# Queries and keys of a prompt attention stored in split form: the split at the eviction, with the sums' scaling on VectorE

## The chip, the cores and the metric

The kernel runs on one core of a Trainium2 chip. The metric is device time in microseconds (us) of one execution, lower is better. The kernel before takes 3180.88 us as the median of 3 runs (3177.26 to 3182.94).

## The reference

One inference step of a decoder layer, all in 32-bit floats: 2048 prompt tokens and 8 x 8 sampled tokens with 8192 cached positions each. One input projection feeds eight heads of attention with a forget gate (FoX) and four heads of a matrix memory (mLSTM); their outputs are mixed by w_o, and a norm, a squared-ReLU MLP and a norm follow. What the change touches is the attention of the prompt:

```python
z  = x @ w_in                                  # 1024 columns in; queries and keys of FoX are 512 each
fq, fk, fv = z[..., :512], z[..., 512:1024], z[..., 1024:1536]      # 8 heads x 64
L  = cumsum(log_sigmoid(forget gate))
s  = (fq . fk) * 64**-0.5 + L[q] - L[k]        # keys up to the query
o  = softmax(s) . fv
# mLSTM, in chunks: C_new = g_state * C + sum(w_key k v),  g_state = exp(...)
mix = concat(o, norm(mLSTM) * og) @ w_o;  x1 = LN(ALPHA*x + mix)
y   = LN(ALPHA*x1 + square(relu(x1 @ w1)) @ w2)
```

`k_prompt`, the plain keys, is one of the outputs.

## The kernel before

**Split products.** TensorE multiplies in a rounded 32-bit form. A product that must be exact is made of parts: ScalarE copies a tile into the rounded form (the high part, `split_hi`, L154), VectorE subtracts it from the tile (the low part, `split_lo`, L157), and TensorE adds the products of the parts (`mm3`, L163 to L165). For the attention's scores a head has only 64 dimensions, so keys stand twice on 128 partitions: the high part in the upper 64 and the low part in the lower 64 of one tile `ks`, and one matmul of 128 partitions multiplies a part of the queries with both parts of the keys. Queries stand twice for this, too, in `qh` and `ql`.

**Stages.** The execution goes through these stages in order.

- `block_a`, four times (512 prompt tokens each, the first with the 64 sampled ones): the input projection in passes of 256 columns. Each pass loads its weights on SP's queue (`wra`), splits them (`whi`, `wlo`), and evicts its banks `pm`. The FoX queries and keys are passes with eight groups j of 128 columns, four of queries, four of keys. ScalarE evicts them in pieces of 256 tokens (L634, queries scaled by 0.125) into one of four buffers `st`, and SP stores them, queries to a scratch `dq`, keys to the output `k_prompt`. In the first block the sampled columns stand ahead of them in a bank of 320.
- `m_block`, woven into the next block's matmuls: the mLSTM chunks of a finished block. Four decays per block come from a scratch `dgs` into `gsb`; ScalarE exponentiates them at L741, ahead of the block's first chunk; the state's update at the end of a chunk uses them.
- the sampled attention, in small steps woven between the other stages' matmuls by `tick`. Its gathers of cached keys and values are DMAs on POOL's queue.
- `phase_b`, the prompt attention: eight heads, one after the other, each in eight units g of 256 queries (two query tiles of 128). `scores` makes a unit's banks `pS` (two matmuls each, `qh` and `ql` against `ks`), and VectorE adds the decay row `nl` and takes the maximum. `values` exponentiates on ScalarE, turns the result on TensorE, and multiplies with the values `vn`. The values of a unit are issued behind the scores of the next (LA = 1). ScalarE and VectorE bring the result into `ot` (L1105, L1107), one buffer of 1024 queries for four units.
- `phase_o`, the output projection with the first norm, then `phase_c`, the MLP. Their rows x come on SP's queue (L1345), as do the mixed rows `xr` (L1318) and the first weights `wr` of w_o (L1247, five of which are loaded in the last units of the attention already).

**The loads of the attention.** All go through SP's queue, in program order. Query tiles (`qn`, 128 x 256, twice the same 64 rows) are loaded two units ahead and split behind the scores of the unit before. The four key pieces of the next head (`kn`, 128 x 512) are loaded in units 0 to 3 (head 0's own and head 1's at other places) and split two units later. The next head's `nl` (1 MB) and `vn` (512 KB) are loaded in unit 3, behind its scores. Beside these, POOL's queue carries the additions `dw` that prepare the MLP's weights (`w2_sum`), with the accumulation done by the DMA; a counter spreads them over the units.

**The end of four units.** `finish` inverts the sums of the exponentials and puts three steps into the list `ends`; each of the next units starts with one of them. `stores` writes the inverses to a scratch (four small DMAs on SP), `sums` reads them back along the queries, on 64 partitions (`rl`, two DMAs), and `scale` multiplies the two halves of `ot` with them on POOL (L1133) and stores them to `dmix` (L1134, SP). For the last four units all steps follow at once: VectorE scales the first half, POOL the second, and POOL's queue stores both. There are two buffers `ot`.

The order of the work is that of the program on each engine; tile pools set when a buffer comes free. DMAs of SP's queue have eight semaphores in turn, so that a DMA also waits for the one eight places ahead of it.

## Time and profile before

| what | value |
|---|---|
| median of 3 runs | 3180.88 us |
| the profiled execution, its own time | 3166.91 us |
| its span in the profile | 3165.1 us, granted clock 0.990 |
| TensorE (PE) busy | 97% of the span |
| VectorE (DVE), ScalarE (ACT), GpSimd (POOL) busy | 67%, 46%, 30% |
| projections and mLSTM, sampled attention beside them | 0 to 865 us |
| prompt attention, eight heads | 865 to 1304.4 us |
| output projection and first norm | 1304.4 to about 1540 us |
| MLP and second norm | the rest |

Times in the trace run from the start of the span. A group of the profile is a line of the program, an engine, an operation, and its tiles as out<-in; busy us and the mean ns of one follow, then the idle time of the engine just ahead of these instructions and what ended it. A matmul's end is modelled, so "busy" TensorE includes matmuls that are a little stretched. The waits have the waiting engine on the left and what it waited for on the right, then us in sum, the count and the longest.

### The profile page before, as it was taken

The page shows a single profiled execution, that of the slowest core. Times are in us where ns is not written, and L with a number is a line of the kernel's source. Part 1 is how long each engine was busy: PE and PEld are TensorE (multiplying, and loading weights), DVE is VectorE, ACT ScalarE, POOL GpSimd, SP SyncE. Part 2 cuts the span into 40 slices and gives each one's busy share as a digit, 9 for nine tenths or more (in the row PEclk, how much of TensorE's full clock was granted, in tenths as well). Part 3 has the DMA queues.
Part 4 walks back from the last instruction along what each step waited for, and adds up shares of the span by engine and source line. Part 5 has one row for each costly group of instructions (what it writes and reads, how often), then busy time and mean ns, then how long its engine had stood idle before and what let it go on. Part 6 is the DMA issues. An engine that isn't in the chain of part 4 may idle for free.

```text
span 3165.1 us, 53757 instructions
## 1 busy us (share of the span) xinstructions
PE 3076.4 (97%) x19713; PEld 2425.7 (77%) x19713; DVE 2125.0 (67%) x5095; ACT 1457.3 (46%) x2648; POOL 961.5 (30%) x1046
## 2 busy tenths in 40 slices
PE   8999999999999999899999999999999999999998
PEld 8997787787766676677777777776777776798886
DVE  6857557466487888544566668665676656787888
ACT  4343244334377777422334354443454444455552
POOL 0121232333333334376423334324333222111110
PEclk9999999999999999999999999999999999999999
DMA  5565775777787787487977778978778866587772
GB/s 193 152 212 179 238 234 188 277 267 250 238 269 196 210 211 172 159 303 261 359 277 271 279 274 302 344 263 315 282 280 325 317 226 238 156 266 200 210 203 77
DMA packets 332512, 765.36 MB, mean 242 GB/s; under 512 B 64057, under 2 KB 154681, under 8 KB 331353
## 3 DMA queue, kind: packets, MB, share of 16 engines
q1 hardware_dynamic: 236120, 414.41, 39.9%
q0 software_dynamic: 90864, 330.61, 31.4%
q10 hardware_dynamic: 5264, 16.91, 1.4%
q8 instruction: 156, 2.56, 0.3%
q14 instruction: 108, 0.88, 0.1%
HBM read 709.23 MB, written 93.98 MB: 254 GB/s over the span
## 4 chain that ended last, share of the span: by engine, by line
PE 76%; DMA 11%; issue 5%; DVE 5%; POOL 2%; ACT 1%; SPq 0%; DVEq 0%; POOLq 0%; ACTq 0%
PE py L163 6%; PE py L165 6%; PE ph L163 6%; PE ph L165 6%; PE py L164 6%; PE ph L164 6%; PE pw L1359 5%; PE pm L163 5%; PE pm L165 5%; PE pm L164 5%; DMA y<-cache_v,idxV 3%; PE sO L2245 3%; PE po L1097 3%; DMA vt<-cache_v,idxV 3%; PE sQ L2132 3%
## 5 line engine op out<-in xcount | busy, mean ns | idle before, releaser
L157 DVE TENSOR_TENSOR wl<-wr,wh 128x1024 fp32r<-128x1024 f32 x321 | 393.5, 1230 | 237.3 <-ACT wh L154 235.7
L154 ACT ACTIVATE wh<-wr 128x1024 fp32r<-128x1024 f32 x321 | 337.6, 1055 | 326.0 <-PE ph L164 168.9
L2109 POOL DMA_INDIRECT kT<-cache_k,idxK x256 | 276.5, 1080 | 642.7 <-PE sQ L2132 576.4
L163 PE MATMUL py<-wh,hh 128*128 128x512 f32 x904 | 357.6, 400 | 0.1
L164 PE MATMUL py<-wl,hh 128*128 128x512 f32 x904 | 353.7, 393 | 0.0
L165 PE MATMUL py<-wh,hl 128*128 128x512 f32 x904 | 352.6, 394 | 0.8 <-DVE hl L157 0.8
L1668 DVE TENSOR_TENSOR y<-y,py 128x512 f32<-128x512 f32 x404 | 272.4, 681 | 84.5 <-PE py L165 81.4
L163 PE MATMUL ph<-x1h,wh 128*128 128x512 f32 x768 | 303.8, 396 | 0.0
L2221 POOL DMA_INDIRECT vt<-cache_v,idxV x197 | 203.2, 1032 | 329.8 <-PE sO L2245 257.4
L164 PE MATMUL ph<-x1l,wh 128*128 128x512 f32 x768 | 301.5, 393 | 0.0
L165 PE MATMUL ph<-x1h,wl 128*128 128x512 f32 x768 | 299.9, 393 | 0.0
L163 PE MATMUL pm<-xh,whi 128*128 128x512 f32 (+2 forms) x640 | 231.0, 361 | 0.0
L165 PE MATMUL pm<-xh,wlo 128*128 128x512 f32 (+2 forms) x640 | 228.8, 357 | 0.0
L164 PE MATMUL pm<-xl,whi 128*128 128x512 f32 (+2 forms) x640 | 227.9, 356 | 0.0
L163 PE MATMUL pm<-whi,xh 128*128 128x256 f32 (+4 forms) x624 | 202.1, 325 | 8.0 <-ACT whi L154 8.0
L157 DVE TENSOR_TENSOR wlo<-wra,whi 128x1024 fp32r<-128x1024 f32 (+1 forms) x112 | 141.0, 1261 | 101.1 <-ACT whi L154 100.8
L163 PEld LDWEIGHTS py<-wh,hh 128*128 128x128 f32 x904 | 169.4, 188 | 50.0 <-issue 5.9
L165 PEld LDWEIGHTS py<-wh,hl 128*128 128x128 f32 x904 | 170.1, 188 | 41.5 <-issue 4.9
L164 PE MATMUL pm<-wlo,xh 128*128 128x256 f32 (+4 forms) x624 | 199.5, 320 | 0.6 <-DVE wlo L157 0.6
L165 PE MATMUL pm<-whi,xl 128*128 128x256 f32 (+4 forms) x624 | 199.9, 320 | 0.0
L164 PEld LDWEIGHTS py<-wl,hh 128*128 128x128 f32 x904 | 170.5, 189 | 35.2 <-issue 2.5
L154 ACT ACTIVATE hh<-hq 128x512 fp32r<-128x512 f32 x150 | 94.1, 631 | 215.4 <-PE py L164 150.6
(442 smaller groups left out, 7210.5 us busy)
## 6 DMA issues: line engine op xcount, KB each, us to landing
wr<-w SPq DMA_DIRECT2D x214, 512.0 KB
wra<-w_in SPq DMA_DIRECT2D x104, 512.0 KB
wr<-dw SPq DMA_DIRECT2D x97, 512.0 KB
dw<-w POOLq DMA_DIRECT2D x63, 512.0 KB, 8.6
wr<-w POOLq DMA_DIRECT2D x34, 512.0 KB, 8.4
Rb<-dR SPq DMA_DIRECT2D x128, 128.0 KB
wx<-dw SPq DMA_DIRECT2D x17, 512.0 KB
xn<-xp_t SPq DMA_DIRECT2D x16, 512.0 KB
```

The costliest lines, as they stand in the source:

```text
L154: last["ACT"] = A.activation(dst, src, AF.Copy, scale=scale)
L157: r = (eng or V).tensor_tensor(dst, src, hi.bitcast(F32), op=OP.subtract)
L163: T.matmul(ps, wh, xh, start=first, stop=False, skip_group_check=shared)
L164: T.matmul(ps, wh, xl, start=False, stop=False, skip_group_check=shared)
L165: last["PE"] = T.matmul(ps, wl, xh, start=False, stop=stop, skip_group_check=shared)
L1097: last["PE"] = T.matmul(po[c:c + 64, q0:], z["vn"][:, k], PTs[k // 4][:, k % 4, q0:], start=(k < 2), stop=(k >= nk - 2), skip_group_check= ...
L1359: last["PE"] = T.matmul(ps, m[t][x][:, k], (wh, wl)[w][hf][k], start=i == 0, stop=i == 23)
L1668: V.tensor_tensor(y, y, ps, op=op)
L2109: G.indirect_dma_start(out=piece(n), out_offset=None, in_=ck, in_offset=IO(ap=idxK[:, b, j // 2, j % 2:j % 2 + 1], axis=0))
L2132: r = T.matmul(pq[h4 * 32:h4 * 32 + 32, hg].rearrange("p (k c) -> p k c", k=2), z["qb"][:, hd], kv, start=(db == 0), stop=(db == 1), skip_ ...
L2221: vx["last"] = G.indirect_dma_start(out=vt.rearrange("p f c -> p (f c)"), out_offset=None, in_=cv, in_offset=IO(ap=idxV[:, b, (kt % 4) * 4 ...
L2245: after_ = T.matmul(po[r:r + 32], z["PT"][:, hg, 2 * f + g, pg].rearrange("p h q -> p (h q)"), vts[f][:, g, hg * 256:(hg + 1) * 256], star ...
```

## The change

The change has four parts.

1. The scratch `dq` becomes two planes, high and low part, and a scratch `dk` of the same form is added for keys. The projection's eviction writes the high part on ScalarE (whole, 512 or 256 columns, L639 of the new program) and the low part on VectorE (`scalar_tensor_tensor`, scale times bank minus high part), and SP stores both. The plain keys are still copied and stored to `k_prompt`. The new tiles share the buffers of two others of that stage (tags `ac` and `qi`).
2. The attention loads finished parts: `ks` in place (high part to the upper, low part to the lower 64 partitions), and one tile `q` of 128 x 2 x 256 with both parts. `split_hi`, `split_lo`, `kn`, `qn`, `qh` and `ql` go. The next head's `nl` and `vn` are loaded in unit 4, behind its scores, no longer in unit 3.
3. VectorE scales all the sums; an empty step stands ahead of `scale` in `ends`, so it comes a unit later; `ot` has three buffers.
4. The exponential of `gsb` is issued behind the first chunk's outputs.

```diff
-    dq = drm.tile([4, 128, S], F32, name="dq")
+    dq = drm.tile([2, 512, S], F32, name="dq")
+    dk = drm.tile([2, 512, S], F32, name="dk")
...
+    def q_of(h, g):
+        return dap(dq, h * 64 * S + g * 256, [[S, 64], [512 * S, 2], [1, 256]])
...
-                for o in range(w % 256, w, 256):
-                    st = pa.tile([128, 256], F32, name="st", bufs=4)
-                    A.activation(st, ps[:, o:o + 256], AF.Copy, scale=scale)
-                    SY.dma_start(O["k_prompt"][jj * 128:(jj + 1) * 128, a:a + 256] if c else dq[jj, :, a:a + 256], st)
+                n = w // 256 * 256
+                hi = pa.tile([128, 512], F32, name="sa", tag="ac", bufs=2)[:, :n].bitcast(F32R)
+                lo = pa.tile([128, 512], F32, name="sq", tag="qi", bufs=2)[:, :n].bitcast(F32R)
+                A.activation(hi, ps[:, w - n:], AF.Copy, scale=scale)
+                V.scalar_tensor_tensor(lo, ps[:, w - n:], scale, hi.bitcast(F32), op0=OP.mult, op1=OP.subtract)
+                for d, x in enumerate((hi, lo)):
+                    SY.dma_start((dk if c else dq)[d, jj * 128:(jj + 1) * 128, a:a + n], x.bitcast(F32))
+                for o in range(w - n, w, 256):
+                    if c:
+                        st = pa.tile([128, 256], F32, name="st", bufs=4)
+                        A.copy(st, ps[:, o:o + 256])
+                        SY.dma_start(O["k_prompt"][jj * 128:(jj + 1) * 128, a:a + 256], st)
                     a += 256
...
-        A.activation(gsb, gsb, AF.Exp)
...
+            if c % 4 == 0:
+                A.activation(gsb, gsb, AF.Exp)
...
+        def keys_load(z, g):
+            h = z["h"]
             for d in range(2):
-                SY.dma_start(kn[d * 64:d * 64 + 64], kp[h * 64:h * 64 + 64, g * 512:(g + 1) * 512])
+                SY.dma_start(z["ks"][g][d * 64:d * 64 + 64].bitcast(F32), dk[d, h * 64:h * 64 + 64, g * 512:(g + 1) * 512])
...
-            k = z["ks"][:, g * 512:(g + 1) * 512]
-            split_hi(k, kn)
-            split_lo(k[64:128], kn[64:128], k[64:128])
...
-            qn = qns.pop() if qns else pb.tile([128, 256], F32, name="qn", bufs=3)
+            q = qs.pop() if qs else pb.tile([128, 2, 256], F32R, name="q", bufs=3)
             for d in range(2):
-                SY.dma_start(qn[d * 64:d * 64 + 64], dq[h // 2, h % 2 * 64:h % 2 * 64 + 64, g * 256:(g + 1) * 256])
+                SY.dma_start(q[d * 64:d * 64 + 64].bitcast(F32), q_of(*units[n]))
...
-            split_hi(qh, qn)
-            split_lo(ql, qn, qh)
...
-                z["ot"] = pb.tile([64, 1024], F32, name="ot", bufs=2)
+                z["ot"] = pb.tile([64, 1024], F32, name="ot", bufs=3)
...
-                    (V if end and q == 0 else G).tensor_tensor(ot[:, s], ot[:, s], rls[q], op=OP.mult)
+                    V.tensor_tensor(ot[:, s], ot[:, s], rls[q], op=OP.mult)
...
-            ends.extend([stores, sums, scale])
+            ends.extend([stores, sums, lambda: None, scale])
...
-                    if g == 3:
-                        forget_values(Z[h + 1], 0, S)
...
+                if h < 7 and g == 4:
+                    forget_values(Z[h + 1], 0, S)
```

**SP's queue inside a head.** The first place is the middle of one head on SP. `kn` and `ks` are key pieces, `qn` and `q` queries, `drl` and `rl` the inverses on their way out and back, `nl` and `vn` the next head's decays and values. Before:

```order
L1122 DMA drl<-lt 8x32 x4
L1010 DMA qn<-dq 64x256 x2
L1128 DMA rl<-drl 64x512 x2
L993 DMA kn<-k_prompt 64x512
L1010 DMA qn<-dq 64x256 x2
L993 DMA kn<-k_prompt 64x512
L993 DMA kn_11817<-k_prompt 64x512
L1134 DMA dmix<-ot 64x512
L993 DMA kn_11817<-k_prompt 64x512
L985 DMA vn_10996<-v_prompt 128x16x64
L1134 DMA dmix<-ot 64x512
L1010 DMA qn<-dq 64x256 x2
```

After:

```order
L1116 DMA drl<-lt 8x32 x4
L1011 DMA q<-dq 64x2x256 x2
L1122 DMA rl<-drl 64x512 x2
L1005 DMA ks_10837<-dk 64x512 x2
L1011 DMA q<-dq 64x2x256 x2
L1005 DMA ks_10837<-dk 64x512 x2
L1128 DMA dmix<-ot 64x512
L999 DMA nl_11088<-dnl 128x2048
L1000 DMA vn_11087<-v_prompt 128x16x64
L1011 DMA q<-dq 64x2x256 x2
L1128 DMA dmix<-ot 64x512
L1011 DMA q<-dq 64x2x256 x2
```

The keys go straight into `ks`, a unit's queries are behind the pair `nl` and `vn`, and the store `dmix` of the scaled sums stands ahead of that pair and behind it, as before it stood around `vn`.

**SP's queue at the start of the output projection.** The second place is where the attention ends, with the waits of each DMA (semaphores by name; those that begin with DMAHW are of SP's own DMAs, DMASW of POOL's queue, Pool and DVE of these engines). `rl` are the last inverses, `y` and `y5` rows of x, `xr` the mixed rows, `wr` weights of w_o. Before:

```order
L1128 DMA rl_15507<-drl_68 64x512 [waits DMAHW2_49,DMAHW3_49,DMAHW1_49,DMAHW0_49]
L1128 DMA rl_15509<-drl_68 64x512 [waits DMAHW5_49]
L1345 DMA y_15561<-x_prompt 128x1024 [waits DMAHW6_49]
L1345 DMA y_15563<-x_prompt 128x1024 [waits DMAHW4_49,DMAHW7_49,DVE_49,PE_49]
L1345 DMA y_15792<-x_prompt 128x1024
L1345 DMA y5_15892<-x_prompt 128x1024 [waits DMAHW5_49,Pool_49]
L1345 DMA y_16007<-x_prompt 128x1024
L1318 DMA xr_9289<-dmix_67 128x8x128 [waits DVE_49]
L1247 DMA wr_15602<-w_o2 128x1024 [waits DVE_49]
L1247 DMA wr_15608<-w_o2 128x1024 [waits DVE_49]
L1247 DMA wr_15614<-w_o2 128x1024 [waits DMAHW6_49,DVE_49]
```

After:

```order
L1122 DMA rl_15301<-drl_69 64x512 [waits DMAHW2_49,DMAHW3_49,DMAHW1_49,DMAHW0_49]
L1122 DMA rl_15303<-drl_69 64x512 [waits DMAHW5_49]
L1331 DMA y_15355<-x_prompt 128x1024 [waits DMAHW6_49,PE_49,Pool_49]
L1331 DMA y_15357<-x_prompt 128x1024 [waits DMAHW4_49,DMASW7_49,DMAHW5_49,DMASW5_49,DMAHW7_49,DMASW4_49,DVE_49]
L1331 DMA y_15586<-x_prompt 128x1024
L1331 DMA y5_15686<-x_prompt 128x1024
L1331 DMA y_15801<-x_prompt 128x1024
L1304 DMA xr_9434<-dmix_68 128x8x128 [waits DVE_49]
L1233 DMA wr_15396<-w_o2 128x1024 [waits DVE_49]
L1233 DMA wr_15402<-w_o2 128x1024 [waits DVE_49]
L1233 DMA wr_15408<-w_o2 128x1024 [waits DMAHW6_49,DVE_49]
```

Before, `y5` waits for POOL; after, the second `y` waits for two DMAs of POOL's queue (DMASW4 and DMASW5, the stores of the scaled sums), and what stands behind it on the queue waits with it.

**ScalarE in the second block.** The third place is the first chunk of mLSTM that runs beside the FoX projection of the second block. `whi` are weights' high parts, `gsb` the decays, `den`, `Wq` and `ot` the chunk's denominators, exponentials and turned outputs, `st` and `sa` evictions. Before:

```order
L154 ACTIVATE whi<-wra 128x1024
L741 ACTIVATE gsb<-gsb 128x16
L753 ACTIVATE den<-gm 128x4 x2
L154 ACTIVATE whi<-wra 128x1024
L634 ACTIVATE st<-pm 128x256 x2
L748 ACTIVATE Wq<-Wq,gm 128x128 x4
L750 ACTIVATE Wq<-Wq 128x512
L698 COPY ot<-mm 128x4x64
L634 ACTIVATE st<-pm 128x256 x2
L154 ACTIVATE whi<-wra 128x1024 x2
L634 ACTIVATE st<-pm 128x256 x2
```

After:

```order
L155 ACTIVATE whi<-wra 128x1024
L794 ACTIVATE gsb<-gsb 128x16
L764 ACTIVATE den<-gm 128x4 x2
L155 ACTIVATE whi<-wra 128x1024
L639 ACTIVATE sa<-pm 128x512
L646 COPY st<-pm 128x256 x2
L710 COPY ot<-mm 128x4x64
L639 ACTIVATE sa<-pm 128x512
L646 COPY st<-pm 128x256 x2
L759 ACTIVATE Wq<-Wq,gm 128x128 x4
L761 ACTIVATE Wq<-Wq 128x512
L155 ACTIVATE whi<-wra 128x1024
```

The exponential of `gsb` stands between the same two loads of weights, and the copy `ot` has moved from behind the exponentials of `Wq` to ahead of them.

More of the change, by code (lines that the diff above doesn't have):

```diff
@@ L229, in begin_b @@
         for d in range(2):
-            for t, x in (("kn", O["k_prompt"][0:64, 0:512]), ("qn", dq[0, 0:64, 0:256])):
-                r = SY.dma_start(bf[t][d * 64:d * 64 + 64], x)
+            for t, x in (("ks", dk[d, 0:64, 0:512]), ("q", q_of(0, 0))):
+                r = SY.dma_start(bf[t][d * 64:d * 64 + 64].bitcast(F32), x)
                 tc.add_manual_dep(r.ins, at,
@@ L970, in bank, with keys_home, head @@
             return ppb.tile([128, 512], F32, name="pS", bufs=2)
[L972 to L979 removed]
+        def keys_home(h):
+            ks = homes.pop(h, None) or pb.tile([128, 2048], F32R, name=f"ks{h % 2}")
+            return dict(h=h, ks=[ks[:, g * 512:g * 512 + 512] for g in range(4)])
+        def head(z):
+            e = z["h"] % 2
+            z["vn"], z["nl"] = homes.pop("vn", None) or (pb.tile([128, 16, 64], F32, name=f"vn{e}"),
+                                                         pb.tile([128, 2048], F32, name=f"nl{e}"))
+            z["ls"] = pb.tile([128, 32], F32, name="ls", bufs=2)
+            G.memset(z["ls"], 1.0)
         def forget_values(z, a, n):
@@ L1041, in scores @@
                     pS = bank()
-                    T.matmul(pS[:, :w], qh[:, qs], ks[:, a:a + w], start=True, stop=False)
-                    last["PE"] = T.matmul(pS[:, :w], ql[:, qs], ks[:, a:a + w], start=False, stop=True)
+                    T.matmul(pS[:, :w], qh[:, qs], z["ks"][a // 512][:, :w], start=True, stop=False)
+                    last["PE"] = T.matmul(pS[:, :w], ql[:, qs], z["ks"][a // 512][:, :w], start=False, stop=True)
                     tick(0.42)
@@ L1153, in phase_b @@
         dmask = bf["mask"]
-        keys(Z[0], 0, bf["kn"])
+        forget_values(Z[0], 0, 512)
         sc = {}
-        qnext = {1: queries_load(1)}
-        knext = {}
+        qnext = {0: bf["q"], 1: queries_load(1)}
         w2_due = [0.0]
```

69 lines of the change are left out of this document (20 added, 49 removed).

## The prediction

> **What bounds the kernel now.** I read the page first, then the busy time by stretches, then the waits inside the attention stage.
>
> ```profile
> span 3165.1 us, 53757 instructions
> PE 3076.4 (97%) x19713; PEld 2425.7 (77%) x19713; DVE 2125.0 (67%) x5095; ACT 1457.3 (46%) x2648; POOL 961.5 (30%) x1046
> ```
>
> TensorE is busy for 97% of the span and the change takes no matmul away. So only idle time of TensorE can be won: 3165.1 - 3076.4 = 88.7 us in all. The next view says where it lies. The stretches are: the projections and mLSTM chunks; the eight heads of the prompt attention, cut where each head's first score matmul starts; the start of the output projection; the rest. Columns: length, then busy us of PE, PEld, DVE, ACT, POOL, then granted clock, DMA share, GB/s.
>
> ```profile
> 0.00:865.00 865.00, 843.36 (x5724) 714.97 (x5724) 536.17 (x1561) 320.02 (x652) 227.65 (x260) 0.99 0.66 221
> 865.00:914.80 49.80, 44.23 (x263) 29.59 (x264) 41.38 (x167) 36.83 (x86) 13.22 (x21) 0.93 0.73 213
> 914.80:969.30 54.50, 51.78 (x361) 36.74 (x360) 42.64 (x171) 40.48 (x96) 25.72 (x39) 1.00 0.86 298
> 969.30:1024.90 55.60, 52.75 (x360) 37.35 (x359) 43.55 (x172) 40.28 (x96) 21.82 (x33) 0.97 0.83 188
> 1024.90:1082.10 57.20, 53.77 (x364) 37.37 (x362) 46.04 (x175) 41.61 (x98) 20.91 (x33) 0.97 0.78 202
> 1082.10:1134.60 52.50, 51.85 (x364) 36.71 (x361) 44.18 (x175) 40.48 (x95) 20.37 (x31) 1.00 0.83 199
> 1134.60:1186.90 52.30, 51.60 (x361) 36.67 (x360) 44.41 (x173) 41.00 (x98) 22.48 (x36) 1.00 0.87 228
> 1186.90:1239.50 52.60, 51.55 (x364) 36.83 (x362) 44.01 (x175) 41.53 (x99) 22.74 (x34) 1.00 0.78 190
> 1239.50:1304.40 64.90, 64.08 (x461) 44.96 (x458) 45.58 (x183) 48.70 (x109) 15.96 (x25) 1.00 0.43 94
> 1304.40:1345.00 40.60, 31.04 (x182) 21.65 (x182) 18.76 (x31) 9.16 (x10) 18.40 (x9) 0.92 0.67 247
> ```
>
> The attention takes 1304.4 - 865 = 439.4 us. Heads 4 to 6 are alike: 52.3 to 52.6 us, TensorE idle for 0.7 to 1.1. Heads 1 to 3 do the same work and are 9.9 us longer together (54.5 + 55.6 + 57.2 - 3 x 52.47). Head 0 is idle for 5.57 us. The 40.6 us behind the attention hold 9.56 us of idle. VectorE is busy for 84% of a steady head (44.2 of 52.5), ScalarE for 78%: near enough to full that latencies reach TensorE, but neither is the bound of heads 4 to 6.
>
> **The attention, part by part.** The change moves the split of queries and keys out of this stage; a head then loads finished parts. These are the groups that leave, ahead of the scaling of the sums, which goes from POOL to VectorE:
>
> ```profile
> L157 DVE TENSOR_TENSOR ql<-qn,qh 128x256 fp32r<-128x256 f32 x64 | 36.6, 579 | 4.1 <-ACT qh L154 3.8
> L157 DVE TENSOR_TENSOR ks<-kn,ks 64x512 fp32r<-64x512 f32 x32 | 23.5, 766 | 0.6
> L154 ACT ACTIVATE qh<-qn 128x256 fp32r<-128x256 f32 x64 | 26.6, 417 | 17.1 <-DMA qn<-dq 7.2 <-PE po L1097 4.9 <-PE pS L1042 3.6
> L154 ACT ACTIVATE ks<-kn 128x512 fp32r<-128x512 f32 x32 | 18.1, 624 | 2.0 <-DMA kn<-k_prompt 2.0
> L1133 POOL TENSOR_TENSOR ot<-ot,rl 64x512 f32<-64x512 f32 x31 | 50.0, 1617 | 128.0 <-DMA rl<-drl 50.0 <-ACT S L1071 36.4 <-ACT PT L1090 28.5
> 1302.41 0.68 DVE L1133 TENSOR_TENSOR ot<-ot,rl 64x512 f32<-64x512 f32 x1 [1.62 <-DMA rl<-drl]
> ```
>
> VectorE: -36.6 - 23.5 + 31 x 0.68 = -39.0 us. ScalarE: -26.6 - 18.1 = -44.7 us. POOL: -50.0 us. All of it lies beside matmuls, so it is worth only the idle it causes. The next rows show how a late scaled sum reaches TensorE (the first has the least, the median and the longest issue of its stores, in ns): with two buffers ot, ScalarE waits for the store of an old one, VectorE behind it, TensorE behind both.
>
> ```profile
> L1134 SPq DMA_DIRECT2D dmix<-ot x30: 460/461/16894, 898.5 to 1279.9; - x30
> ACT ot L1105 <- DMA dmix<-ot: 5.0, 1, 5.0
> PE po L1097 <- DVE ot L1107: 2.7, 1, 2.7
> 1010.00:1015.00 5.00, 3.79 (x27) 2.63 (x23) 0.51 (x4) 0.64 (x2) 0.00 (x0) 1.00 1.04 228
> 1015.00:1020.00 5.00, 3.47 (x17) 1.94 (x18) 3.50 (x11) 3.51 (x8) 0.50 (x1) 0.66 0.29 89
> ```
>
> One store took 16.89 us to issue where 0.46 is the median, and the two stretches around the stall lose 1.21 + 1.53 us of matmul time; the second runs at clock 0.66. The third ot removes this wait. Heads 1 to 3 can give back 0 to 9.9 us; I take 8, nearer to the steady heads, since the path that stalled them goes. Head 0: 0 to 5.57; I take 4, because the splits stood between its first loads and its matmuls, but TensorE now waits for those loads itself. Heads 4 to 7: idle 0.65 + 0.70 + 1.05 + 0.82 = 3.2 us at most; I take 2. Sum -14. The Trainium skill (TensorE: Matmul & The Clock Gate, Part 1) says that an idle window of about 3.4 us halves the clock until as long a busy one; the 0.66 agrees. By that rule every long stall that goes saves about 1.7 us more, which the length of heads 2 and 3 already holds, so the sum stays.
>
> **The start of the output projection.**
>
> ```profile
> 1305.11 0.42 DVE L1107 TENSOR_TENSOR ot<-ot,po 64x256 f32<-64x256 f32 x1
> L1133 POOL TENSOR_TENSOR ot<-ot,rl x31: 1266/1279/9036, 897.2 to 1305.6; 64x512 f32<-64x512 f32 x31
> 1306.60 4.62 DVE L157 TENSOR_TENSOR wl<-wr,wh 128x1024 fp32r<-128x1024 f32 x4
> SPq L1345 <- POOL ot L1133: 10.6, 1, 10.6
> 1316.01 2.44 SPq L1247 DMA_DIRECT2D wr<-w_o  x3
> PE pw L1359 <- ACT woh L154: 8.9, 1, 8.9
> dmix<-ot POOLq DMA_DIRECT2D x1, 128.0 KB, 4.7
> 1315.82 1.05 POOL L2221 DMA_INDIRECT vx<-cache_v,idxV  x1 [0.31 <-issue]
> ```
>
> The last scaling, at 1305.6, took 9.04 us on POOL where the median is 1.28. A load of x (L1345) waited 10.6 us for it, the loads of w_o stood behind on SP's queue until 1316.01, and TensorE idled 8.9 us for them. After, VectorE does it: 1305.11 + 0.42 + 0.68 = 1306.2. But the order shows that the second load of x now waits for the store of the scaled sums instead. So: 1306.2, plus 4.7 to landing, plus four loads and one of the mixed rows at about 0.46 each (an estimate from the median issue of the stores above) = 1313.2, against 1316.0: 2.8 us won, not 8.9. POOL's gathers, which shared the DMA engines with these loads from 1315.8 on, start some 8 us sooner; two more loads of x (1 MB, 3.5 us at the 298 GB/s of head 1) now stand ahead of w_o. Bounds 0 to 8.9; I take -4, nearer to the 2.8. The Trainium skill (SBUF — State Buffer, SBUF: two separate sides) says that a VectorE operation with two SBUF inputs and a GpSimd operation that reads SBUF lock each other out; the 9.04 us beside four such subtractions (wl) agrees. By it the move to VectorE pays in the heads too, at most the 1617 - 1279 = 338 ns that the POOL rows run over, 31 x 0.338 = 10 us, off the critical path: no change of the sum.
>
> **The projections.**
>
> ```profile
> L634 ACT ACTIVATE st<-pm 128x256 f32<-128x256 f32 x64 | 21.4, 376 | 48.9 <-PE pm L165 16.6 <-issue 12.5 <-DVE qr L627 9.9
> L1364 DVE SCALAR_TENSOR_TENSOR y<-y,pw x32: 667/687/689, 1313.5 to 1534.6; 128x512 f32<-128x512 f32 x32
> L642 ACT COPY sa<-pm 128x512 f32<-128x512 f32 x5 | 2.9, 583 | 0.0
> GB/s 193 152 212 179 238 234 188 277 267 250 238 269 196 210 211 172 159 303 261 359 277 271 279 274 302 344 263 315 282 280 325 317 226 238 156 266 200 210 203 77
> 745.00:790.00 45.00, 45.00 (x299) 35.67 (x298) 23.74 (x72) 20.36 (x50) 14.91 (x20) 1.00 0.78 281
> ACT gsb L741 <- DMA gsb<-dgs: 6.0, 1, 6.0
> PE mm L769 <- ACT ot L698: 3.0, 1, 3.0
> ```
>
> There are 40 evictions: 16 of 256 columns in the first block, 24 of 512. ScalarE before: 64 x 0.376 = 24.1 us. After: 16 x 0.376 + 24 x 0.583 for the high parts, 32 x 0.376 for the plain keys = 32.0: +7.9. VectorE: no row has a 256-wide one from these banks; at half of 0.687 to all of it, 40 low parts are 22 to 27 us more. Both lie under matmuls: in 745 to 790 TensorE is busy for 45.0 of 45.0 us and VectorE for 23.74. If that cover fails, a late eviction costs at most its own 0.687 us, 27 us in all. Written bytes go from 8 to 20 MB; at 281 GB/s in this stretch, with 3 MB more per block in about 60 us (+50 GB/s), they stay below the 344 that the page has as the mean of a whole slice of 79 us. SP's queue gets 112 stores for 64, and weight loads stand behind them. I take +1 (0 to +6). The later exponential: ScalarE's 6.0 us wait for gsb stays where it stands in block 1 (the order has it at the same weights), but the copy ot, for which TensorE idled 3.0 us, now stands ahead of the Wq exponentials: -3 (0 to -3). Sum -2.
>
> **The sum.** -14 - 4 - 2 = -20 us. The profiled execution took 3166.9 us (span 3165.1 and 1.8 around it), so 3146.9 by it. The median of the timed runs, 3180.9, lies 14.0 above; I carry that over: 3161.
>
> **The rivals.**
>
> ```profile
> qn<-dq SPq DMA_DIRECT2D x126, 64.0 KB
> ACT S L1071 <- DVE mx L1057: 44.0, 50, 3.0
> ```
>
> *Queries late (slower).* A load of queries is now 128 KB, and TensorE waits for it directly. In each of seven heads it stands on SP's queue right behind the next head's nl (1 MB) and vn (512 KB in 256-byte rows). From that place to its use are the scores of two units (12 of a head's 40 banks) and the values of two (18 of 72 key tiles): about 0.27 x 52.5 = 14 us, an estimate. The nl takes 5 us at 199 GB/s, and behind a vn the queue stood for up to 16.89: 22 us, so 8 late, 7 x 8 = 56, less the 20: 3217. It decides from 20 / 7 = 2.9 us late per head. For it: DMA share of 1.04 in the stalled stretch. Against: one head in three had such a block, and without the waits on POOL the w2 additions that filled the engines come less in bursts. The Trainium skill (DMA: Bandwidth & Descriptors, Queues, rings and completion order) says that each engine takes turns between queues by packets: small packets then stand behind other queues' large ones. By that the late case is the rule; the heads without a block speak against it. Chance 0.10.
>
> *Engines bound the steady heads (faster).* ScalarE waited 44.0 us in 50 waits for the maximum; a busy TensorE is a modelled busy. If 39 us less on VectorE packs matmuls tighter, by 2.5 of 52.5 us per head, the eight give 20 more: 3141. For it: VectorE's 84%. Against: 0.7 us of idle. Chance 0.20.
>
> *It does little.* DMA bursts still stretch heads 1 to 3 (+8), w_o lands no sooner (+4), the projections gain nothing (+2): -6, 3175. Chance 0.15.
>
> **The numbers.** The forecast has 0.55; its own range, from its terms' bounds, is 3150 to 3173. About 0.2% (6.4 us) is what a measurement of this kernel can tell from no change. Faster: 0.55 + 0.20 = 0.75; the third rival sits at the edge and is counted as same: 0.15; slower 0.10. The range takes in the faster and the small case and leaves out the late one: 3140 to 3178.
>
> **What would show it.** Right: heads 1 to 3 within 1 us of heads 4 to 6; no wait of ScalarE for the store of ot; no POOL row for the scaled sums; w_o's loads near 1313 less the earlier gain; the idle before woh at 4 to 6 us. Wrong: waits of TensorE's weight loads for DMA q above 3 us per head; steady heads at 50 us or less; VectorE waiting for rl; or a projection stage that is longer than 865 us by more than 5.

## The result and the profile after

The changed kernel takes 3262.21 us as the median of 6 runs (3249.83 to 3301.25), against 3178.41 for the kernel before (6 runs, 3174.79 to 3182.94). That is 83.8 us slower, where 20 us faster had been forecast. One of the six executions (3301.25) ran at a granted clock of 0.91 where the others had 0.98; without it the median is 3259.60, 81.2 us slower, and the ratio 1.0254, with a 95% interval of 1.0234 to 1.0275. The profiled execution took 3259.6 us.

First the page of the changed kernel, the span and the engines' busy times:

```profile
span 3257.9 us, 53634 instructions
PE 3103.7 (95%) x19713; PEld 2440.5 (75%) x19713; DVE 2104.9 (65%) x5070; ACT 1431.1 (44%) x2560; POOL 923.6 (28%) x1015
```

VectorE, ScalarE and POOL have less to do than before (2125.0, 1457.3 and 961.5 us), as the change meant. TensorE is idle for 154 us instead of 89. The next view cuts the execution at the same places as the prediction did: the projections, the eight heads, the start of the output projection (columns as there).

```profile
0.00:872.20 872.20, 848.06 (x5722) 714.58 (x5723) 551.48 (x1599) 326.77 (x657) 235.20 (x258) 0.99 0.70 233
872.20:926.10 53.90, 44.17 (x270) 31.72 (x269) 35.97 (x153) 30.50 (x69) 10.44 (x21) 0.91 0.75 229
926.10:983.80 57.70, 52.91 (x362) 37.50 (x361) 39.77 (x165) 36.91 (x85) 20.10 (x35) 0.97 0.82 270
983.80:1055.10 71.30, 54.12 (x357) 38.06 (x356) 39.30 (x165) 37.38 (x86) 16.83 (x29) 0.88 0.71 168
1055.10:1115.80 60.70, 53.37 (x362) 37.76 (x361) 39.64 (x164) 36.88 (x85) 15.41 (x29) 0.97 0.80 203
1115.80:1184.00 68.20, 53.66 (x358) 38.60 (x357) 39.21 (x163) 37.13 (x85) 16.05 (x29) 0.87 0.72 178
1184.00:1247.50 63.50, 55.77 (x361) 39.48 (x360) 39.88 (x165) 37.23 (x85) 15.48 (x29) 0.92 0.75 191
1247.50:1317.70 70.20, 55.83 (x362) 39.63 (x362) 39.73 (x165) 37.37 (x85) 16.79 (x30) 0.88 0.71 174
1317.70:1388.00 70.30, 64.65 (x463) 46.75 (x461) 44.91 (x180) 47.02 (x102) 10.79 (x21) 0.95 0.41 93
1388.00:1430.00 42.00, 40.94 (x239) 30.09 (x235) 23.64 (x40) 12.07 (x14) 26.16 (x17) 1.00 0.95 341
```

The projections end 7.3 us later. The attention takes 1388.0 - 872.2 = 515.8 us instead of 439.4: this is the loss, 76.4 us, and all heads have a part of it, also the steady ones of before (52.3 to 52.6 us each, now 63.5 to 70.2). VectorE's busy time per head fell from 44 to 40 us, yet TensorE idles for 5 to 17 us per head, and its clock falls to 0.87 in the worst. The start of the output projection is better than before: 1.06 us idle in 42, where 9.56 in 40.6 were.

Who waits in the attention (865 to 1400 us)? The waits of VectorE, TensorE and POOL, and in the second fence one of SP's queue:

```profile
POOL nd L1029 <- DVE mx L1048: 300.3, 69, 16.4
...
DVE ot L1127 <- DMA rl<-drl: 63.8, 12, 9.5
...
PE pS L1036 <- DMA q<-dq: 33.6, 7, 12.1
...
PE pS L1036 <- DMA drl<-lt: 13.4, 1, 13.4
```

```profile
SPq L1011 <- PE pS L1037: 94.9, 20, 13.1
```

Three things are new. VectorE waits 63.8 us for the inverse sums `rl`; POOL had waited 50.0 us for them before, beside the path. TensorE waits for queries (the stall of 13.4 us, which the profile puts down to a store `drl`, is in head 2 and is one of these, as shown below). And SP waits 94.9 us for TensorE's scores before it can load queries: the buffer `q` that a load fills is read by the score matmuls themselves, where the old `qn` was free once it was split, a unit earlier. Two places show how each wait is paid. On VectorE, in head 3:

```profile
1066.31 0.15 DVE L1066 TENSOR_REDUCE ls<-lp 128x1 f32<-128x1 f32 x1
1075.99 0.68 DVE L1127 TENSOR_TENSOR ot<-ot,rl 64x512 f32<-64x512 f32 x1 [9.53 <-DMA rl<-drl]
1076.59 0.68 DVE L1044 CUSTOM_DVE_ANT_0 S<-pS,nl 128x512 f32<-128x512 f32 x1
```

A scaling of 0.68 us holds VectorE for 9.53 us, and the maxima of the scores, which everything else needs, stand behind it. On SP's queue, in head 2 (the issue time is the second column):

```profile
1003.65 0.35 SPq L999 DMA_DIRECT2D nl<-dnl  x1
1005.03 0.41 SPq L1000 DMA_DIRECT2D vn<-v_prompt  x1
1005.54 12.77 SPq L1011 DMA_DIRECT2D q<-dq  x2
1018.42 2.26 SPq L1128 DMA_DIRECT2D dmix<-ot  x1
```

The queries of unit 6 stand behind `vn` for 12.77 us. The scores of unit 5 end at 1019.4, those of unit 6 begin at 1032.8, and between 1020 and 1030 TensorE does nothing, at a clock that falls to half:

```profile
1020.00:1025.00 5.00, 0.00 (x0) 0.00 (x0) 0.46 (x2) 0.10 (x1) 0.00 (x0) 0.76 1.07 222
1025.00:1030.00 5.00, 0.00 (x0) 0.00 (x0) 0.00 (x0) 0.00 (x0) 0.00 (x0) 0.50 1.06 224
```

The DMA engines are full there (1.06). What fills them is told by the queues' shares between 1005 and 1036 us (packets, MB, share of the 16 engines' time):

```profile
q0 software_dynamic: 1008, 3.67, 59.4%
q1 hardware_dynamic: 3446, 2.82, 31.7%
```

POOL's queue, which carries the additions `dw` of the MLP's weights, takes nearly twice the time of SP's.

### The profile page after: what moved, and what is told of

It reads as the page before. It is cut to its first block, busy times and chain, and to the rows that moved or that the text cites. A ratio compares the mean times of both kernels' runs of the same rounds, so it can differ in the third digit from the quotient of the medians.

```text
span 3257.9 us, 53634 instructions
## 1 busy us (share of the span) xinstructions
PE 3103.7 (95%) x19713; PEld 2440.5 (75%) x19713; DVE 2104.9 (65%) x5070; ACT 1431.1 (44%) x2560; POOL 923.6 (28%) x1015
## 4 chain that ended last, share of the span: by engine, by line
PE 71%; DMA 15%; issue 5%; DVE 4%; POOL 2%; ACT 1%; SPq 1%; another core or an unknown queue 1%; DVEq 0%; ACTq 0%; POOLq 0%
PE py L164 6%; PE py L166 6%; PE py L165 6%; PE ph L164 5%; PE ph L166 5%; PE ph L165 5%; PE pw L1345 5%; PE pm L164 4%; PE pm L166 4%; PE pm L165 4%; PE sQ L2118 3%; PE sO L2231 3%; DMA vt<-cache_v,idxV 3%; DMA q<-dq 3%; PE po L1091 2%
## 5 line engine op out<-in xcount | busy, mean ns | idle before, releaser
L1044 DVE CUSTOM_DVE_ANT_0 S<-pS,nl 128x512 f32<-128x512 f32 (+3 forms) x288 | 167.5, 595 | 90.8 <-PE pt L1081 46.2
L1065 ACT ACTIVATE S<-S,mx 128x1024 f32<-128x1024 f32 (+2 forms) x192 | 171.6, 895 | 89.1 <-DVE mx L1051 72.3
L1036 PE MATMUL pS<-ks,q 128*128 128x512 f32 (+2 forms) x320 | 143.2, 450 | 66.7 <-DMA q<-dq 33.6
```

Of the source, the lines that this page charges most:

```text
L1036: T.matmul(pS[:, :w], qh[:, qs], z["ks"][a // 512][:, :w], start=True, stop=False)
L1044: last["DVE"] = V.tensor_tensor_reduce(out=sp[:, :e - a], in0=pS[:, :e - a], in1=nl[:, a:e], scale=1.0, scalar=NEG, op0=OP.add, op1=OP.max ...
L1065: last["ACT"] = A.activation(sp[:, :w], sp[:, :w], AF.Exp, bias=mx[:, 7:8], accum_out=lp[:, k:k + 1])
```

## The experiments

Each run was timed beside the kernel before on the same chip; chips differ by up to 0.6%, so the table gives differences of medians on one chip. Attention is the time from the first score matmul to the first matmul of the output projection in the run's profile, "start" the first of these two times, and "O" the time of the output projection's first 96 matmuls. The rest of the execution, with the same code in all, took between 1814 and 1845 us from one profiled execution to the next (1821 in the one of the kernel before, 1840 in the changed kernel's; 1814 to 1825 on three of the chips, 1834 to 1845 on two), so that a single profile is read by these three columns. Their differences add up to the timed difference within 8 us, but for e8, whose profiled execution was 12.6 us above its median: there they give 48 us. Absolute times in the expectations count from the 3178 us of the kernel before.

The traces also show the order of the operations on each engine and on SP's queue, and a scheduler makes it: it is not everywhere that of the program's text. So one edit can change much else. In the attention, e6 differs from the kernel before by its one operation alone, e14 from e13 by the places of loads on SP's queue alone, and e17 from e14 by a few neighbours. e9, e10, e11, e12, e16 and e15 have the order of the run that they start from (e15 that of e3), so they are repeats of e3, e7, e6, e1, e14 and e3. The others, e13 among them, have another kind of operation (scores, turning or values) at 184 to 1321 of TensorE's 2880 places in the attention.

| run | us against before | ratio, 95% interval | attention | start | O |
|---|---|---|---|---|---|
| kernel before | 0 | | 439.6 | 864.9 | 39.3 |
| changed kernel | +81.2 | 1.0234 to 1.0275 | 516.0 | 872.2 | 29.2 |
| e1_q5: five buffers q | +78.0 | 1.0186 to 1.0274 | 517.6 | 873.7 | 29.1 |
| e2_pool: POOL scales | +47.9 | 1.0108 to 1.0182 | 491.3 | 875.5 | 29.1 |
| e3_q5pool: both | +14.8 | 1.0028 to 1.0055 | 463.2 | 873.7 | 29.1 |
| e4_nl3: nl, vn a unit earlier | +71.6 | 1.0199 to 1.0246 | 521.5 | 872.0 | 29.1 |
| e5_proj: before + the projection's part | +10.9 | 1.0008 to 1.0052 | 433.9 | 875.2 | 40.8 |
| e6_last: before + last scaling on VectorE | -13.3 | 0.9931 to 0.9970 | 440.6 | 860.6 | 29.1 |
| e7_bvec: before + all scalings on VectorE | +61.3 | 1.0157 to 1.0223 | 509.0 | 862.8 | 29.1 |
| e8_qn2: before, two buffers qn | +28.9 | 1.0052 to 1.0116 | 478.8 | 869.6 | 43.2 |
| e9_early: e3 + sums to be stored earlier | +11.0 | 1.0017 to 1.0054 | 461.0 | 871.5 | 29.1 |
| e10_bvecearly: e7 + sums to be stored earlier | +56.6 | 1.0144 to 1.0200 | 515.2 | 863.2 | 29.1 |
| e11_lastearly: e6 + sums to be stored earlier | -15.4 | 0.9936 to 0.9977 | 436.1 | 861.0 | 29.1 |
| e12_q5early: e1 + sums to be stored earlier | +61.7 | 1.0176 to 1.0235 | 510.7 | 871.3 | 29.1 |
| e13_pin: scaling held at its place | +35.6 | 1.0083 to 1.0141 | 475.8 | 870.9 | 30.8 |
| e14_q5pin: e13 + five buffers q | +21.5 | 1.0040 to 1.0088 | 461.0 | 872.9 | 30.3 |
| e15_q5pinpool: e3, scaling to be held | +16.6 | 1.0036 to 1.0078 | 458.1 | 870.4 | 29.1 |
| e16_q5pinearly: e14 + sums to be stored earlier | +28.7 | 1.0052 to 1.0106 | 467.2 | 872.5 | 30.0 |
| e17_q5pinhalf: e14, half the query bytes | -0.2 | 0.9975 to 1.0009 | 432.5 | 876.0 | 31.1 |
| e18_half: changed kernel, half the query bytes | +48.8 | 1.0128 to 1.0186 | 485.6 | 871.3 | 29.1 |

### The first four: two causes that hide each other

**e1_q5**

```diff
-            q = qs.pop() if qs else pb.tile([128, 2, 256], F32R, name="q", bufs=3)
+            q = qs.pop() if qs else pb.tile([128, 2, 256], F32R, name="q", bufs=5)
```

> The changed kernel with five buffers q instead of three, nothing else. Theory A (queries late): with three buffers the load of a unit's queries waits until TensorE has done the scores of the unit before (SP waits 94.9 us for that, 20 times), so the pair nl and vn gets ahead of it in SP's queue, and TensorE then waits 13.7, 12.5 and 10.8 us in heads 2, 4 and 6. A expects these three stalls to go and most waits of TensorE for q with them: about 3215 to 3230 us. Theory B (VectorE waits for the inverse sums rl, 63.8 us in 12 waits, with ScalarE and TensorE behind it) expects these waits to stay and no more than 10 us: 3250 to 3262.

The waits of TensorE for queries went from 33.6 to 2.5 us, as theory A said, and the attention did not get shorter (517.6 us, 510.7 in the repeat e12). Its waits in the attention:

```profile
DVE ot L1127 <- DMA rl<-drl: 105.1, 15, 13.5
...
PE pS L1036 <- DMA q<-dq: 2.5, 1, 2.5
```

VectorE's waits for `rl` grew by 41 us in their place. A likely reason, not tried by itself, is that the loads that come earlier are ahead of the sums on the queue.

**e2_pool**

```diff
-                    V.tensor_tensor(ot[:, s], ot[:, s], rls[q], op=OP.mult)
+                    (V if end else G).tensor_tensor(ot[:, s], ot[:, s], rls[q], op=OP.mult)
```

> The changed kernel with POOL scaling the sums, as before the change, except for the last four units, where VectorE still scales both halves. Theory B expects that POOL takes over the wait for rl (about 60 us), that no VectorE wait for it stays, and 30 to 55 us less: 3207 to 3232. Theory A expects the long waits for queries to stay and at most 15 us less: 3247 to 3262.

33 us came back, in the range of theory B. The waits for queries grew instead, as e1's grew for the sums:

```profile
POOL ot L1127 <- DMA rl<-drl: 58.3, 8, 10.5
PE pS L1036 <- DMA q<-dq: 55.9, 16, 13.3
```

**e3_q5pool** has both edits.

> Five buffers q and POOL's scaling together. If A and B each hold a part, the gains add up, and the attention comes back to its length before (439 us) or below: 3165 to 3185. If the extra bytes of the split parts are the cause by themselves, whoever waits, more than 20 us stay: above 3195.

Together they win 66 us where alone they win 3 (20 in the repeat e12) and 33. 14.8 us stay, and 23.6 us of the attention, so one part was still missing. POOL's and VectorE's waits point at one place:

```profile
POOL ot L1127 <- DMA rl<-drl: 146.7, 12, 19.3
...
DVE S L1048 <- POOL nd L1029: 47.5, 11, 8.0
```

The masks `nd` stand behind POOL's waiting scalings, and VectorE waits 47.5 us for these.

**e4_nl3**

```diff
-                if h < 7 and g == 4:
+                if h < 7 and g == 3:
                     forget_values(Z[h + 1], 0, S)
```

> The changed kernel with the pair nl and vn loaded in unit 3, where it was loaded before the change. Theory C (it is the place of the pair that makes the queries late) expects the stalls of 10 to 14 us to go: about 3225. Theory A expects the pair to stand ahead of the queries of another unit instead, with stalls of the same kind there: 3250 to 3275.

The attention did not get shorter (521.5 us), and TensorE's waits for queries are 42.3 us in 8. Theory C falls: wherever the pair stands, the queries of some unit stand behind it.

### The parts of the change alone, on the kernel before

**e5_proj**

```diff
+                A.activation(hi, ps[:, w - n:], AF.Copy, scale=scale)
+                V.scalar_tensor_tensor(lo, ps[:, w - n:], scale, hi.bitcast(F32), op0=OP.mult, op1=OP.subtract)
+                for d, x in enumerate((hi, lo)):
+                    SY.dma_start((dk if c else dqs)[d, jj * 128:(jj + 1) * 128, a:a + n], x.bitcast(F32))
                 for o in range(w % 256, w, 256):
```

> The kernel before with the projection's part alone: the high and low parts are made and stored to two scratch tensors that nobody reads, with the change's tiles and lines, and the queries and keys are evicted and stored as before as well. (Queries are evicted once more than in the changed kernel.) The changed kernel reached its attention 7.3 us later than the kernel before. If the evictions cause that (ScalarE and VectorE waiting for the two buffers of the high and low parts, 8.2 us for dq<-sq in the first block), this kernel is 5 to 12 us slower than before. If the later exponential of gsb causes it, the difference is below 2 us.

10.9 us slower, with the attention starting at 875.2: the evictions alone give the projections' loss. In the changed kernel most of it lies in the first block. The stretch of 150 to 170 us, before and after:

```profile
150.00:170.00 20.00, 20.00 (x159) 20.00 (x158) 16.90 (x67) 6.16 (x14) 3.38 (x3) 1.00 0.76 221
```

```profile
150.00:170.00 20.00, 15.37 (x119) 14.87 (x118) 16.74 (x53) 3.70 (x7) 2.35 (x2) 1.00 0.57 178
```

and two waits of the changed kernel between 130 and 200 us:

```profile
DVE sq L640 <- DMA dq<-sq: 8.2, 3, 3.5
ACT st L646 <- DVE sq L640: 7.4, 4, 3.5
```

TensorE loses 4.6 of the 20 us. VectorE, busy for 0.85 of its time there before, waits for the stores of the two low-part buffers, and ScalarE's evictions wait behind it.

**e6_last**

```diff
-                    (V if end and q == 0 else G).tensor_tensor(ot[:, s], ot[:, s], rls[q], op=OP.mult)
+                    (V if end else G).tensor_tensor(ot[:, s], ot[:, s], rls[q], op=OP.mult)
```

> The kernel before with one edit: VectorE scales both halves of the last four units' sums, where POOL scaled the second. In the changed kernel the output projection's first 96 matmuls took 29.2 us against 39.3. If this edit is the cause by itself, this kernel is 9 to 10 us faster than before, and POOL's 9.04 us and TensorE's 8.9 us wait for w_o go. The prediction's step (2.8 us by the store's landing, 4 taken) expects 3 to 4.

13.3 us faster. The first 96 matmuls of the output projection take 29.1 us, as in the changed kernel. In the changed kernel's timeline the loads of w_o issue 1392.68 - 1388.0 = 4.7 us behind the start of the last value matmul, where it was 1316.01 - 1304.2 = 11.8:

```profile
1388.41 3.40 SPq L1331 DMA_DIRECT2D y<-x_prompt  x5
1391.86 0.78 SPq L1304 DMA_DIRECT2D xr<-dmix  x1
1392.68 4.85 SPq L1233 DMA_DIRECT2D wr<-w_o  x3
```

**e7_bvec** has `V.tensor_tensor` in that line, for all units.

> The kernel before with VectorE scaling all the sums, at the place where POOL did it (no empty step, two buffers ot, queries and keys split in the attention). Theory B says that a wait for rl on VectorE costs TensorE time wherever it is: POOL waited 50.0 us in 7 waits for rl, so VectorE waits about as long, and the attention grows by 15 to 35 us, less 9 to 10 at the start of the output projection: 5 to 25 us slower. If rl is only late because of the changed loads, VectorE hardly waits, and the kernel is 5 to 15 us faster.

61.3 us slower, far beyond the upper end of 25: this one engine's choice, with the new order that the scheduler made for it, costs the kernel before 69 us of attention, nearly as much as the change. Its waits from 865 to 1400 us:

```profile
DVE ot L1133 <- DMA rl<-drl: 87.9, 14, 13.8
```

**e8_qn2**

```diff
-            qn = qns.pop() if qns else pb.tile([128, 256], F32, name="qn", bufs=3)
+            qn = qns.pop() if qns else pb.tile([128, 256], F32, name="qn", bufs=2)
```

> The kernel before with two buffers qn instead of three, so that the load of a unit's queries waits about as long as in the changed kernel, with half its bytes. Theory A (the lead in units that was lost) expects waits of ScalarE's split for qn that reach TensorE, as the queries did in the changed kernel with POOL's scaling (attention 28 us longer than with five buffers): 15 to 30 us slower. If the doubled bytes matter and not the lead, less than 5 us.

28.9 us slower. A unit less of lead costs that with the old bytes (and the order that came with it):

```profile
ACT qh L154 <- DMA qn<-dq: 71.2, 18, 12.1
```

### Why the sums are late

**e9_early**, **e10_bvecearly**, **e11_lastearly** and **e12_q5early** were to store the inverse sums at the end of four units at once, e9 on e3, e10 on e7, e11 on e6, e12 on e1.

```diff
-            ends.extend([stores, sums, lambda: None, scale])
+            stores()
+            ends.extend([sums, lambda: None, lambda: None, scale])
```

(In the two that start from the kernel before, the list is `[sums, lambda: None, scale]`.)

> The changed kernel with five buffers q, POOL's scaling, and the inverse sums stored at once at the end of four units instead of a unit later (and read back a unit earlier, scaled at the same unit). With five buffers and POOL alone, POOL still waited 146.7 us for rl, 12 times, with the masks nd behind it, and the attention took 463.2 us against 439.6. If the late rl is the rest of the loss, the attention comes to 430 to 445 us, and the kernel within 5 us of the kernel before on either side. If the doubled bytes of the queries fill the DMA engines, the attention stays above 455 us and the kernel 10 us or more slower than before.

> The kernel before with VectorE scaling all the sums, as in the run that was 61 us slower, and the inverse sums stored and read back one unit earlier. Theory B (what costs is that VectorE waits for rl, 78.4 us in 12 waits of 6.5 us on average, and not the 0.68 us of the scaling) expects most of that to go, since a unit of 3 to 10 us is won: 0 to 20 us slower than before. If VectorE's work or its place between the scores is the cost, 50 us or more stay.

> The kernel before with VectorE scaling both halves of the last four units (13.3 us faster in the run of that alone), and the inverse sums stored and read back one unit earlier, scaled by POOL otherwise. POOL's 50.0 us of waits for rl should shrink, and with them the late stores of ot that stalled head 2 or 3: 13 to 20 us faster than before. If these waits were off the path, 13.

> The changed kernel with five buffers q and the inverse sums stored and read back one unit earlier; VectorE scales, as in the change. If both causes are mended by this (lead of the queries, lead of rl), it is 10 us slower to 5 us faster than before. If VectorE must not wait for a small load at all, its waits for rl stay above 30 us and the kernel 20 us or more slower.

The intervals of e9, e10, e11 and e12 overlap those of e3, e7, e6 and e1, and what e9, e10 and e12 were to win from early sums did not come. But the edit sent no sums earlier. `finish` is the last thing of one unit and the step `stores` the first of the next, so the stores were at this place already; and the read-back, written a unit earlier, stands where it stood. All DMAs of SP's queue and all operations of the attention on every engine have the same order with the edit as without. So these runs say nothing for or against early sums. As repeats they show how far one program's runs lie apart on two chips: 2.2 to 6.9 us of attention and 2.1 to 16.3 us of the timed difference. SP's queue at one of the places, first e7's, then e10's:

```profile
1011.09 9.94 SPq L1122 DMA_DIRECT2D drl<-lt  x4
```

```profile
996.61 0.54 SPq L985 DMA_DIRECT2D vn<-v_prompt  x1
998.26 10.65 SPq L1134 DMA_DIRECT2D dmix<-ot  x1
...
1011.89 9.87 SPq L1122 DMA_DIRECT2D drl<-lt  x4
1022.71 1.09 SPq L1128 DMA_DIRECT2D rl<-drl  x2
```

and on VectorE in e10:

```profile
1025.71 0.68 DVE L1133 TENSOR_TENSOR ot<-ot,rl 64x512 f32<-64x512 f32 x1 [13.94 <-DMA rl<-drl]
```

SP's queue stands for 10.65 and 9.87 us behind a `vn`, as it stood for 16.89 in the kernel before; there POOL waited behind it, and ScalarE for 5.0 us. The scaling's own place is another matter. The order of VectorE shows how many query tiles stand between an inverse and its two scalings (the first five inverses):

```
changed kernel             3 4 | 4 5 | 5 5 | 2 4 | 4 4
e13, scaling held back     6 6 | 4 5 | 6 6 | 4 4 | 6 6
```

The empty step does not do what it says: in the changed kernel the scaling stands 2 to 5 tiles behind the inverse, not 6. That the scheduler takes `rl` for landed early is the likely reason and is not shown.

**e13_pin**

```diff
-                    V.tensor_tensor(ot[:, s], ot[:, s], rls[q], op=OP.mult)
+                    with tc.issue_after(last["DVE"].ins):
+                        V.tensor_tensor(ot[:, s], ot[:, s], rls[q], op=OP.mult)
```

> The changed kernel with one edit: the scaling on VectorE is held behind the last scores of the unit ahead of its step, so that its place is the one that the empty step asks for (6 query tiles behind the inverse, where the scheduler had put it 2 to 5 behind). Theory B' (VectorE waits for rl because the scheduler moved the scaling ahead, to where it took rl for landed) expects VectorE's waits for rl to fall from 63.8 us to below 20, and the kernel to be as slow as with POOL's scaling or less: 25 to 50 us slower than before, with the waits for queries left. If the place on VectorE does not matter, it stays 70 us or more slower.

46 us came back, 40 of them in the attention, and the queries' waits stay. The edit is this one line, but the scheduler ordered much of the attention anew with it (1321 of its 2880 matmuls and transposes on TensorE have another kind in their place), so the place of the scaling is not parted from the rest of that order. What speaks for it is that VectorE's waits for `rl` fell by about as much, to 17.5 us up to 1340 us and to 22.0 up to 1400, with the last scaling:

```profile
PE pS L1036 <- DMA q<-dq: 35.8, 14, 6.4
...
DVE ot L1128 <- DMA rl<-drl: 17.5, 7, 7.0
```

Of these 17.5 us, nothing lies at the 16 scalings that stand 6 tiles behind their inverse. All of it lies at the second inverse of a head, where the held scaling still stands 4 behind.

**e14_q5pin** has five buffers q as well, **e15_q5pinpool** POOL's scaling besides (e3 with the hold).

> The same with five buffers q. If lateness of rl at its early place and the lost lead of the queries are the whole loss of the attention, the attention takes 432 to 445 us (439.6 before), and the kernel is 5 us faster to 8 us slower than before: the projections' 9 us lost, the 10 us at the start of the output projection won. If the doubled bytes are a cause by themselves, the attention stays above 455.

> The same with five buffers q, the scaling held back, and POOL doing it (but for the last four units). The masks nd stood behind POOL's waits for rl (146.7 us in 12, without holding back); if that is the rest of the 23.6 us that the attention lost there, it comes to 432 to 445 us. A difference of more than 3 us to the run with VectorE scaling at the same place tells what the engine itself is worth; expected is none.

The attention comes to 461.0 us, above the 455 at which the doubled bytes were to be suspected; VectorE waits for `rl` 36.5 us, 12 times, of which 31.4 are again at the scalings 4 tiles behind and 0.6 at those 6 behind. e15 (458.1) missed its 432 to 445. On POOL the hold changed no order, so it is e3 once more: POOL waits 136.5 us for `rl` and VectorE 43.4 for the masks. With five buffers, the held scaling on VectorE and POOL's at its own place come out alike (461.0 and 467.2 against 463.2, 461.0 and 458.1): VectorE as such is not the cost.

### What is left: the bytes

**e16_q5pinearly** is e14 with the sums to be stored earlier. **e17_q5pinhalf** and **e18_half** leave the low parts of the queries in DRAM, e17 on e14, e18 on the changed kernel:

```diff
-                SY.dma_start(q[d * 64:d * 64 + 64].bitcast(F32), q_of(*units[n]))
+                SY.dma_start(q[d * 64:d * 64 + 64, 0].bitcast(F32), q_of(*units[n])[:, 0])
...
-            qh, ql = q[:, 0], q[:, 1]
+            qh, ql = q[:, 0], q[:, 0]
```

> The changed kernel with five buffers q, the scaling held behind the scores of the unit ahead of its step, and the inverse sums stored and read back a unit earlier. With five buffers and the held scaling VectorE still waited 36.5 us for rl in 12 waits, and the attention took 461 us. If the late rl is what is left, the waits fall below 15 us and the attention to 435 to 448 us. If rl is late by the DMA queue itself, whenever it is asked for, the waits stay above 25 us and the attention above 455.

> Five buffers q and the held scaling, and the low parts of the queries are not loaded (64 KB a load as before the change, instead of 128; the second score matmul takes the high part again, so that the output is not the reference's). If the doubled bytes of the queries make rl late and are the rest of the loss, the attention comes from 461 us to 435 to 448. If the order on SP's queue does it by itself, it stays above 455.

> The changed kernel with the low parts of the queries not loaded, as in the run ahead of this, and nothing else changed: three buffers q, VectorE's scaling where the scheduler put it. If bytes are the common cause, 40 us or more of the 84 go. If the lost lead and the place of the scaling are, at most 20 us go, and VectorE's waits for rl stay above 50 us.

e16 has the order of e14 (39.4 us of waits, attention 467.2), so whether the sums are asked for too late stays open. e17 brought the attention to 432.5 us, 7 below the kernel before and just below the 435 to 448 expected, and VectorE's waits to

```profile
DVE ot L1128 <- DMA rl<-drl: 20.2, 10, 5.6
```

e18 lies between its two expectations: 32 us of the 81 go, with VectorE's waits for `rl` as long as before (63.4 us) and those for queries halved (16.7). So the bytes are a part of the loss and not the common cause of it. (With its bytes a load loses half its rows, too; these runs do not part the two.)

Step by step the attention goes 516.0, 475.8 (scaling held), 461.0 (queries' lead restored; 467.2 in the repeat e16), 432.5 (half the bytes): 40, 9 to 15, and 28 to 35 us. The three together are the whole loss of the attention. Their shares are less sure: with the scaling in its early place, five buffers win next to nothing, and 16 of the last step's 28 us are waits for `rl`, at 4 tiles behind, which a longer hold might have taken as well. That was not tried.

## Why the prediction was wrong

**The scaling on VectorE.** The step that failed is the sum on VectorE, "-36.6 - 23.5 + 31 x 0.68 = -39.0", with all of it "beside matmuls". It moved the work of an operation and left out what the operation waits for. The row that it quoted had the number: POOL's 31 scalings were idle for 50.0 us for `rl`. On POOL little waited behind it (VectorE 1.9 us for POOL's masks); VectorE is in the loop of scores, maximum and exponential, and TensorE pays for its waits. The runs put 40 us of attention on it (e13, with 42 us less of these waits), and 69 in the kernel before (e7, with 87.9 us of waits), each with the order that came with the edit. The text named "VectorE waiting for rl" as a sign of being wrong, and gave it no price and no chance. It also took the empty step at its word: the order of the changed kernel had the scaling 2 to 5 query tiles behind the inverse, and it was not read there.

**The third ot.** "The third ot removes this wait" held: ScalarE no longer waits for a store of `ot`. What had delayed that store, SP's queue behind `vn`, stayed, and it now delays the queries and the sums. Heads 1 to 3, which were to give 8 us, take 22.4 more (3.2 + 15.7 + 3.5), head 0 takes 4.1 more where 4 were to come, and heads 4 to 7 take 49.9 more.

**Queries late.** This rival had the right mechanism and the right place (in heads 2, 4 and 6 the queries of unit 6 stand behind `nl` and `vn`, and TensorE is idle for 13.4, 12.1 and 10.4 us ahead of that unit's scores), at a chance of 0.10 and a price of 56 us. It had missed why there is no cover: the lead. A load of queries now waits for the scores of three units earlier in its buffer, which e8 prices at 29 us with the old bytes and e14 at 9 to 15 us. Its argument against, that the additions `dw` would come less in bursts, failed: seven of them (3.67 MB) lie in the stall of 1005 to 1036, as many as were issued from 991 to 1001 at the stall of the kernel before. The Trainium skill (DMA: Bandwidth & Descriptors, Queues, rings and completion order) has each DMA engine take turns between queues by packets, and the prediction said itself that by this the late case is the rule. The trace fits in that the loads of one unit's queries took 12.77 us to issue where POOL's queue had 59.4% of the engines' time; that the turns hold up the issue is not shown. A run without the additions was not made, so their share is argued and not shown.

**Bytes.** The prediction looked at the added bytes of the projections, by mean rates; in the attention it doubled the load of queries and priced this in the rival alone. The queries' second half costs 28 to 35 us of attention in e17 (22 to 29 timed) and 30 in e18 (32 timed).

**The clock.** The stalls are longer than the half-clock window that the Trainium skill states (TensorE: Matmul & The Clock Gate, Part 1), and the trace agrees: 0.50 in the second 5 us without a matmul. Busy time in heads 4 to 6 rose from 51.6 to 51.9 us to 53.7 to 55.8, so by an estimate 2 to 4 us of their loss are slow matmuls and not idle time.

**The output projection.** Right in kind, mis-sized: 4 us taken, 10 measured (39.3 to 29.2 us; e6 alone 39.3 to 29.1). The step that failed read the second load of x as waiting for the last store of the sums, at 4.7 us. The two stores issued at 1387.3 and 1390.3:

```profile
L1128 POOL DMA_DIRECT2D dmix<-ot x2: 567/578/588, 1387.3 to 1390.3; - x2
```

The second load of x issued at 1390.01, ahead of the second store, as soon as VectorE's second scaling ended (1389.98), and all five had issued by 1388.41 + 3.40 = 1391.81. So no load of x waited for the second store, and the second load waited for the first only if that landed within 2.7 us. What released it was the scaling itself; the semaphores DMASW4 and DMASW5 in the order were read wrongly as the two stores.

**The projections.** +1 (0 to +6) for the evictions, 7.3 measured, and 10.9 with them alone in e5. The stretch from which their cover was read, 745 to 790 us, is one where VectorE is busy for half its time. In the first block it is at 0.85, and there it was lost. The later exponential did what was said: TensorE's 3.0 us wait for the copy `ot` is gone from the list of waits. It is not seen in the time and was not tried by itself.

The fastest kernel here is the one before with the last scaling on VectorE (e6, 0.9931 to 0.9970, and its repeat e11, 0.9936 to 0.9977). It beats both. No version with split parts in DRAM and all their bytes came below the kernel before.

## What to carry to other kernels

When an operation moves from an engine with slack to one in the loop, its price can be the wait ahead of it on the old engine (50.0 us here) and not its duration; read that wait, and read in the order of the new program where a scheduler has put it. Read the order again before the time of any run is explained: six runs here asked for another order and got the old one. When a copy between a load and its user goes, the load's buffer lives longer, and its lead shrinks by a step: count buffers again. And a second half of bytes on a queue that already stands for 10 us at a time is paid in part by the small transfers behind it (16 of 28 us here).

## What the runs showed of the hardware

- One issue of a DMA held SP's queue for 17.4 us, a quarter of the head that it was in (head 6, 70.2 us). The loads of queries of the changed kernel (least, median and longest issue, ns):

```profile
L1011 SPq DMA_DIRECT2D q<-dq x126: 573/606/17373, 860.9 to 1348.7; - x126
```

- The way of 4 KB of sums through DRAM and back to 64 partitions, four stores and two loads, took 20 us in e10 (from the inverse's turn at 1005.3 to 1025.7). SP's queue was issuing for nearly all of it: the last 3.6 us of a store `dmix`, then queries, then the stores `drl` for 9.87 us.
